# Eight column blocks in PSUM at once for the first products of a two-layer encoder, slice by slice of the depth, with no GpSimd work

## The chip, the cores and the metric

The kernel runs on one core of a Trainium2 chip. The time is the device time of one execution in microseconds (us); the time before is the median of three runs, 1584.74 us (1583.31 to 1587.51).

## The reference, cut to what matters

The model is a two-layer encoder trunk over 256 tokens of width 1024 in float32. Each layer has a feed-forward half step, a mixer of three branches and a second feed-forward half step. Each of the three is fed by a normalised and modulated input. The modulation is a product of a conditioning vector with a large weight matrix `ada_w`.

```python
cs = jax.nn.silu(c)                                   # c: (1, 1024)
mod = cs @ ada_w[l] + ada_b[l]                        # nine vectors of 1024
sh1, sc1, gt1, sh2, sc2, gt2, sh3, sc3, gt3 = jnp.split(mod, 9, axis=-1)
h = rmsnorm(x, norm_gains[l, 0]) * (1 + sc1) + sh1
gate, up = jnp.split(h @ ffn_wi[l, 0], 2, axis=-1)    # 1024 -> 2 x 2816
x = x + 0.5 * gt1 * ((jax.nn.silu(gate) * up) @ ffn_wo[l, 0])
h = rmsnorm(x, norm_gains[l, 1]) * (1 + sc2) + sh2    # the mixer's input
```

## The kernel before, in words

Everything is kept transposed: depth on the partitions, 256 tokens along the free dimension. The depth of 1024 is eight slices k of 128. The 2816 columns of `gate` and of `up` are 22 column blocks j of 128. Each product of a 128x128 weight tile with a slice of the activations is three matmuls (`mm3`, lines 396 to 398), since both factors are split into a rounded high part and the remainder, hi and lo. ScalarE rounds the weights to the high part, VectorE subtracts to get the low part.

The order of the instructions on each engine is written by a planner in the kernel itself (class `Order`). The kernel is a set of Python generators. Each says on which engine it wants to work and how long that takes by the planner's own figures (`yield on("DVE", 1.13)`), which events it waits for, and which counted buffers it takes. The thread that could start first goes first, and among equals the one with the lower priority number. What comes out is a fixed order per engine; on the chip each engine runs its list in order and waits by semaphores. The load queue (SP) is such a list too, planned at 1.45 us a load, landing 2 us after.

The first products, lines 682 to 783, are h @ ffn_wi for the first `NJ0` = 6 column blocks of layer 0, which run while the modulation of this very input is still being computed. For slice k, `ada_w` blocks k (shift) and 8+k (scale) of 128x1024 are needed, 512 KB each, multiplied with the replicated conditioning vector `csb` and summed along the row. VectorE does this for the scales and for shift 7 (line 460, one fused instruction with a reading of its accumulator). For the other seven shifts GpSimd multiplies (line 700) and ScalarE sums (line 702). The list `FIRST` gives the order of the loads: a single number k is the pair of modulation blocks of a slice (shift first, scale second, except for slice 7), a pair (j, q) is half q of the depth, four slices, of column block j with its gate and up columns, 512 KB. So a column block is usable for slices 0 to 3 when its first half has come, and for 4 to 7 when its second has. `first_put` (line 736) multiplies x with the row norm (line 740), applies scale and shift on ScalarE (line 744), and rounds and subtracts in `ha.put` (lines 419, 421). Each pair (slice, block) is multiplied, six triplets a slice for gate and six for up, as soon as both its inputs are planned to be there. The six blocks take six of the eight PSUM banks.

After the first products `ffn` goes on with the other column blocks through the stream `wraw`, `whi`, `wlo` (lines 337, 352, 361), into the PSUM tiles `pmain`. At the end of the first products it also starts the `ada` thread: 24 further modulation blocks, layer 0's vectors 2, 4 and 3, at 12, 17, 22 ... us of planner time after that moment (`FSTART`, `FPACE`). Vector 3 comes last. It is the shift of the mixer's input: `Stats.scale` waits for all of it (line 521), writes it into two extra columns of the early activations (lines 525, 526), and only then sets `e_x`, for which every early product of the mixer waits (`Stats.early`, line 536; the products into `pearly`).

Of the kernel before, what the change touches and what calls it, by code (L numbers as in the profile page):

```python
# [9 lines left out]
F32R = mybir.dt.float32r  # L10
I32 = mybir.dt.int32
U8 = mybir.dt.uint8
AF = mybir.ActivationFunctionType
OP = mybir.AluOpType

L, D, S, H, HD, W = 2, 1024, 256, 8, 64, 512
KT = D // 128
# [8 lines left out]
NRAW, NSPL, NADA, NPM = 3, 4, 2, 3  # L26
ORDER = "cabAgB"
NCK, NLR = 2, 2
WARM = 0
NJ0, SHV = 6, (7,)  # L30
FIRST = ((0,), (0, 0), (1, 0), (2, 0), (3, 0), (4, 0), (1,), (5, 0), (2,), (0, 1), (1, 1), (3,), (2, 1), (3, 1), (4,), (4, 1), (5,), (5, 1), (6,), (7,))
NXF, NXM = 4, 8
PACE, START = 7, 110
FPACE, FSTART = 5, 12
# [1 line left out]
LAT, MM = {"PE": 0.2, "ACT": 0.15, "DVE": 0.13, "SP": 0.0}, 0.329  # L36
# [122 lines left out]
def on(eng, dur, lat=None, tab=None):  # L159
    return ("on", eng, dur, LAT[eng if isinstance(eng, str) else eng[0]] if lat is None else lat, tab)  # L160


def wait(ev):
    return ("wait", ev, 0, 0)
# [6 lines left out]
def take(sem, n=1):  # L171
    return ("take", sem, n, 0)
# [15 lines left out]
def trunk(ctx, tc, A, out):  # L188
    nc = tc.nc
    V, S_, P = nc.vector, nc.scalar, nc.tensor  # L190
# [7 lines left out]
    od = Order()  # L198
    s_raw, s_spl, s_ada = Sem(NRAW), Sem(NSPL), Sem(NADA)
    s_pm, s_px, s_big = Sem(NPM), Sem(8 - NPM), Sem(NBIG)  # L200
# [6 lines left out]
    def paux(name, shape=(128, 512)):  # L207
        return ps.tile(list(shape), F32, name=name, tag="bank", bufs=8)

    def big(name, shape=(128, 4, S), dt=F32):  # L210
        return act.tile(list(shape), dt, name=name, tag="b4", bufs=NBIG)
# [7 lines left out]
    def free_big(n=1):  # L219
        od.release(s_big, n)  # L220


    def cload(key, shape, dt=F32, eng=nc.scalar):
        t = const.tile(list(shape), dt, name="c_" + key)
        eng.dma_start(t, A[key])
        return t

    xT = act.tile([128, KT, S], F32, name="xT")
    csb = const.tile([128, D], F32, name="csb")
# [5 lines left out]
    ada_b = cload("ada_b", [128, L, 72])  # L235
# [11 lines left out]
    for q in range(2):  # L247
        p = paux("pc")
# [58 lines left out]
    for l in range(L):  # L307
# [6 lines left out]
        for q in ORDER:  # L314
            t, b0, b1 = parts[q]
# [79 lines left out]
    def mm3(o, w, xh, xl, first, last):  # L395
        P.matmul(o, w[0], xh, start=first, stop=False)  # L396
        P.matmul(o, w[0], xl, start=False, stop=False)  # L397
        P.matmul(o, w[1], xh, start=False, stop=last)  # L398
# [52 lines left out]
    modT = [const.tile([128, 72], F32, name=f"modT{l}") for l in range(L)]  # L451
# [3 lines left out]
    have1 = [Event() for _ in range(16)]  # L455

    def ada_block(l, blk, raw, got, paced):
        yield wait(got)
        yield on("DVE", 1.14)
        V.tensor_tensor_reduce(out=raw, in0=raw, in1=csb, scale=0.5, scalar=0.0, op0=OP.mult, op1=OP.add,  # L460
                               accum_out=modT[l][:, blk:blk + 1])
        free_big()
        if paced:
            od.release(s_ada)
        v = blk // 8
        if l == 0 and v < 2:
            yield on("DVE", 0.07)
            m, b = modT[0][:, blk:blk + 1], ada_b[:, 0, blk:blk + 1]
            if v == 0:
                V.tensor_add(m, m, b)  # L470
            else:
                V.scalar_tensor_tensor(m, m, b, gains[:, 0, blk - 8:blk - 7], op0=OP.add, op1=OP.mult)
            od.set(have1[blk])
            return
        left[l, v] -= 1
        if left[l, v] == 0:
            yield on("DVE", 0.08)
            V.tensor_add(mod(l, v), mod(l, v), ada_b[:, l, v * 8:v * 8 + 8])
            od.set(have[l, v])

    def ada_load(l, blk, prio, paced=True):
        if paced:
            yield take(s_ada)
        yield take(s_big)
        raw = big("araw", (128, D))
        yield on("SP", 1.45, 0.0)
        nc.sync.dma_start(raw, A["ada_w"][l, blk])
        got = Event()
        od.set(got, 2.0)
        od.spawn(ada_block(l, blk, raw, got, paced), prio)  # L490
# [152 lines left out]
    def ffn_evac(j, p, za, sem=s_pm):  # L643
        yield take(s_z)
        z = small("ffz")
        yield on("ACT", 0.264, tab="exp")
        S_.activation(z, p[:, 0], AF.Tanh, scale=0.5)
        yield on("DVE", 0.34)
        V.scalar_tensor_tensor(z, z, 1.0, p[:, 0], op0=OP.add, op1=OP.mult)
        yield on("DVE", 0.34)  # L650
        V.tensor_mul(z, z, p[:, 1])  # L651
        od.release(sem)
        yield from za.put(j, z)
        od.release(s_z)
# [24 lines left out]
        yield from za.put(j, z)  # L679
        od.release(s_z, 3)  # L680

    w0 = {(j, q): Event() for j in range(NJ0) for q in range(2)}
    raws0 = {q: Event() for q in w0}

    def first_weights(j, q, raw):
        yield take(s_big, 2)
        hi, lo = (big("w0" + n, (128, 2, 512), F32R) for n in "hl")
        yield wait(raws0[j, q])
        yield on("ACT", 0.94)
        S_.copy(hi, raw)  # L690
        yield on("DVE", 1.13)
        V.tensor_tensor(lo, raw, hi, op=OP.subtract)
        free_big()
        w0[j, q].w = hi, lo
        od.set(w0[j, q])

    def first_shift(k, raw, got):
        yield wait(got)
        yield on("POOL", 2.3, 0.2)
        nc.gpsimd.tensor_tensor(out=raw, in0=raw, in1=csb, op=OP.mult)  # L700
        yield on("ACT", 1.05)
        S_.activation(raw, raw, AF.Copy, scale=0.5, accum_out=modT[0][:, k:k + 1])
        free_big()
        yield on("DVE", 0.07)
        V.tensor_add(modT[0][:, k:k + 1], modT[0][:, k:k + 1], ada_b[:, 0, k:k + 1])
        od.set(have1[k])

    def first_mod(k):
        if k in SHV:
            yield from ada_load(0, k, 1, False)  # L710
            yield from ada_load(0, 8 + k, 1, False)
            return
        yield take(s_big)
        raw, got = big("raw0", (128, D)), Event()
        yield on("SP", 1.45, 0.0)
        nc.sync.dma_start(raw, A["ada_w"][0, k])
        od.set(got, 2.0)
        od.spawn(first_shift(k, raw, got), 1)
        yield from ada_load(0, 8 + k, 1, False)

    def first_loads():

        for x in FIRST:
            if len(x) == 1:
                yield from first_mod(x[0])
                continue
            j, q = x
            yield take(s_big)
            raw = big("w0raw", (128, 2, 512))
            yield on("SP", 1.45, 0.0)  # L730
            nc.sync.dma_start(raw, A["ffn_wi"][0, 0, j].rearrange("p (s q c) -> p s q c", s=2, q=2)[:, :, q])
            od.set(raws0[j, q], 2.0)
            od.spawn(first_weights(j, q, raw), 2)
        od.set(e_w)

    def first_put(k, ha):
        yield take(s_z)
        t = small("ht")
        yield on("DVE", 0.34)
        V.tensor_mul(t, xT[:, k], first.r)  # L740
        yield wait(have1[8 + k])
        yield wait(have1[k])
        yield on("ACT", 0.4)
        S_.activation(t, t, AF.Identity, scale=modT[0][:, 8 + k:9 + k], bias=modT[0][:, k:k + 1])
        yield from ha.put(k, t)
        od.release(s_z)

    def first_modulated(ha):
        yield on("DVE", 0.07)
# [4 lines left out]
        first.used()  # L754

    def first_products(ha):

        sems = [s_px] * min(NJ0, 4) + [s_pm] * (NJ0 - 4)
        for q in sems:
            yield take(q)  # L760
        ps0, za = [paux("pfirst", (128, 2, 256)) for _ in range(NJ0)], None
        at_ = {tuple(x): i for i, x in enumerate(FIRST)}
        jobs = sorted((max(at_[k,], at_[j, k // 4]), k, j) for k in range(KT) for j in range(NJ0))
        n, left0 = [0] * NJ0, [4 * NJ0] * 2
        for _, k, j in jobs:
            n[j] += 1
            if k == KT - 1 and za is None:
                yield take(s_big, 12)
                za = Act("z", NJ)
            yield wait(w0[j, k // 4])  # L770
            hi, lo = w0[j, k // 4].w
            for s in range(2):
                c = slice(k % 4 * 128, k % 4 * 128 + 128)
                if ha.ev[k].t is None or ha.ev[k].t > od.cur.t:
                    yield wait(ha.ev[k])
                yield on("PE", MM, 0.0)
                mm3(ps0[j][:, s], (hi[:, s, c], lo[:, s, c]), ha.hi(k), ha.lo(k), n[j] == 1 and s == 0, n[j] == KT and s == 1)
            if n[j] == KT:
                od.spawn(ffn_evac(j, ps0[j], za, sems[j]), 1)
            left0[k // 4] -= 1  # L780
            if left0[k // 4] == 0:
                free_big(2 * NJ0)
        return za

    def ffn(l, f, n, st, lvs, nxt):
# [973 lines left out]
    first = Stats((0, 0))  # L1759
# [148 lines left out]
```

## Time and profile before

| what | us |
|---|---|
| median of three runs | 1584.74 |
| the profiled execution's own time | 1586.35 |
| its span, first to last instruction | 1584.6 |
| TensorE busy in the span | 1533.1 (97%) |
| VectorE busy | 1311.7 (83%) |
| ScalarE busy | 897.0 (57%) |
| GpSimd busy | 21.3 (1%) |

The times in all views are us from the start of the span. A view of windows gives for each engine the busy time in a stretch (x is the number of instructions), then the TensorE clock granted by the throttle as a share of 2.4 GHz, then the load of the DMA engines and what they moved. PE is TensorE, DVE is VectorE, ACT is ScalarE, POOL is GpSimd, SPq the load queue. A duration of an instruction includes its fill; instructions overlap, so the step from one start to the next is what an instruction costs in a row of them.

### The profile page before, as it was taken

How to read it: one execution, taken by the hardware profiler on the slowest of the kernel's cores; microseconds unless marked ns; L12 is line 12 of the kernel's file. 1: busy time of each engine (PE TensorE's matmuls, PEld its weight loads, DVE VectorE, ACT ScalarE, POOL GpSimd, SP SyncE). 2: the span in 40 equal slices, each digit the busy share in tenths (PEclk: the TensorE clock that was granted, in tenths of full speed). 3: DMA queues.
4: the chain of work that ended last, by engine and by line, in shares of the span. 5: the costliest groups of instructions: out<-in, count | busy, mean ns of one | idle time of the engine just before them, and what ended most of it. 6: DMA issues, size and time to landing. Idle time of an engine off the chain costs nothing.

```text
span 1584.6 us, 36797 instructions
## 1 busy us (share of the span) xinstructions
PE 1533.1 (97%) x14518; PEld 1450.6 (92%) x14518; DVE 1311.7 (83%) x2938; ACT 897.0 (57%) x1854; POOL 21.3 (1%) x29
## 2 busy tenths in 40 slices
PE   3999999999999989999999999999999999999998
PEld 3999999988888889999999999998888987999997
DVE  7878889989888869997779877898888896888664
ACT  4655567576554447554565545676655445565554
POOL 3100000000000000000000000000000000000000
PEclk7999999999999989999999999999999999899999
DMA  8588864545464225888657876544446422467553
GB/s 310 188 293 272 284 230 163 180 130 198 140 230 140 74 80 174 277 287 273 226 200 272 285 266 203 185 159 155 160 159 232 168 102 68 136 202 274 184 184 127
DMA packets 91621, 311.61 MB, mean 197 GB/s; under 512 B 11444, under 2 KB 14772, under 8 KB 91448
## 3 DMA queue, kind: packets, MB, share of 16 engines
q1 hardware_dynamic: 91160, 309.15, 57.8%
q8 instruction: 114, 1.87, 0.5%
q14 instruction: 59, 0.48, 0.1%
q10 hardware_dynamic: 288, 0.10, 0.0%
HBM read 308.17 MB, written 1.05 MB: 195 GB/s over the span
## 4 chain that ended last, share of the span: by engine, by line
PE 88%; DMA 5%; DVE 4%; issue 1%; ACT 1%; SPq 0%; DVEq 0%; ACTq 0%
PE pmain L396 21%; PE pmain L397 20%; PE pmain L398 20%; DMA araw<-in_ada_w_dram 5%; PE pearly L396 2%; PE pearly L398 2%; PE pearly L397 2%; PE pX L1175 2%; PE pT L1186 2%; PE pG L1158 1%; PE pS L1488 1%; PE po L1528 1%; DVE wlo L361 1%; PE pmain L1645 1%; PE pmain L1647 1%
## 5 line engine op out<-in xcount | busy, mean ns | idle before, releaser
L352 ACT CAST whi<-wraw 128x512 fp32r<-128x512 f32 x836 | 511.9, 619 | 427.3 <-PE pmain L397 256.0
L361 DVE TENSOR_TENSOR wlo<-wraw,whi 128x512 fp32r<-128x512 f32 x836 | 571.7, 688 | 118.7 <-ACT whi L352 109.2
L396 PE MATMUL pmain<-h,whi 128*128 128x256 f32 x1872 | 539.2, 288 | 0.0
L398 PE MATMUL pmain<-h,wlo 128*128 128x256 f32 x1872 | 525.2, 281 | 1.1 <-DVE wlo L361 1.1
L397 PE MATMUL pmain<-h,whi 128*128 128x256 f32 x1872 | 525.2, 281 | 0.0
L396 PEld LDWEIGHTS pmain<-h,whi 128*128 128x128 f32 x1872 | 351.7, 188 | 13.3 <-issue 4.6
L398 PEld LDWEIGHTS pmain<-h,wlo 128*128 128x128 f32 x1872 | 352.2, 188 | 1.6 <-DVE wlo L361 1.6
L397 PEld LDWEIGHTS pmain<-h,whi 128*128 128x128 f32 x1872 | 352.3, 188 | 0.4
L460 DVE CUSTOM_DVE_ANT_0 araw<-araw,csb 128x1024 f32<-128x1024 f32 x137 | 169.0, 1235 | 47.6 <-DMA araw<-in_ada_w_dram 47.2
L398 PE MATMUL pmain<-z,wlo 128*128 128x256 f32 x704 | 198.2, 282 | 3.4 <-DVE wlo L361 3.3
L397 PE MATMUL pmain<-z,whi 128*128 128x256 f32 x704 | 197.9, 281 | 0.0
L396 PE MATMUL pmain<-z,whi 128*128 128x256 f32 x704 | 197.8, 281 | 0.0
L398 PEld LDWEIGHTS pmain<-z,wlo 128*128 128x128 f32 x704 | 132.6, 188 | 4.4 <-DVE wlo L361 4.2
L396 PEld LDWEIGHTS pmain<-z,whi 128*128 128x128 f32 x704 | 132.6, 188 | 0.0
L397 PEld LDWEIGHTS pmain<-z,whi 128*128 128x128 f32 x704 | 132.6, 188 | 0.0
L396 PE MATMUL pearly<-xh,whi 128*128 128x258 f32 x320 | 91.4, 286 | 0.0
L398 PE MATMUL pearly<-xh,wlo 128*128 128x258 f32 x320 | 90.4, 282 | 0.0
L397 PE MATMUL pearly<-xl,whi 128*128 128x258 f32 x320 | 90.2, 282 | 0.0
L397 PEld LDWEIGHTS pearly<-xl,whi 128*128 128x128 f32 x320 | 60.6, 189 | 0.0
L396 PEld LDWEIGHTS pearly<-xh,whi 128*128 128x128 f32 x320 | 60.4, 189 | 0.0
L398 PEld LDWEIGHTS pearly<-xh,wlo 128*128 128x128 f32 x320 | 60.3, 189 | 0.0
L419 ACT CAST z<-ffz 128x256 fp32r<-128x256 f32 x76 | 30.7, 405 | 40.3 <-DVE ffz L651 39.9
(306 smaller groups left out, 2459.2 us busy)
## 6 DMA issues: line engine op xcount, KB each, us to landing
wraw<-in_ffn_wi_dram SPq DMA_DIRECT2D x164, 512.0 KB, 4.9
araw<-in_ada_w_dram SPq DMA_DIRECT2D x137, 512.0 KB, 6.4
wraw<-in_ffn_wo_dram SPq DMA_DIRECT2D x88, 512.0 KB, 4.5
wraw<-in_w_in_dram SPq DMA_DIRECT2D x78, 512.0 KB, 3.7
wraw<-in_w_gb_dram SPq DMA_DIRECT2D x72, 512.0 KB, 4.2
wraw<-in_w_out_dram SPq DMA_DIRECT2D x16, 512.0 KB, 3.6
w0raw<-in_ffn_wi_dram SPq DMA_DIRECT2D x12, 512.0 KB, 9.8
raw<-in_ada_w_dram SPq DMA_DIRECT2D x7, 512.0 KB, 7.9
```

The source lines that it names most:

```text
L352: S_.copy(hi, part(q))
L361: V.tensor_tensor(lo, part(q), hi, op=OP.subtract)
L396: P.matmul(o, w[0], xh, start=first, stop=False)
L397: P.matmul(o, w[0], xl, start=False, stop=False)
L398: P.matmul(o, w[1], xh, start=False, stop=last)
L419: S_.copy(self.hi(k), src)
L460: V.tensor_tensor_reduce(out=raw, in0=raw, in1=csb, scale=0.5, scalar=0.0, op0=OP.mult, op1=OP.add, accum_out=modT[l][:, blk:blk + 1])
L1158: P.matmul(pp[b][:, i], BK[d][i // 2][hs, i % 2, c].rearrange("p a b -> p (a b)"), ar_view(d, i // 2)[hs, :, i % 2, cs_], start=True, stop ...
L1175: P.matmul(px[half(h), h // 2], G[half(h), h // 2, h % 2, 0:64], T[half(h), h // 2], start=True, stop=True)
L1186: P.matmul(pt[half(h), h // 2], X[half(h), h // 2], TT[half(h), h // 2], start=True, stop=True)
L1488: P.matmul(pS[e][:, t], qT[half(e), hp, t * 128:(t + 1) * 128], kT[half(e), hp], start=True, stop=True)
L1528: P.matmul(po[half(e)], vv[:, j, (2 * hp + e) * 64:(2 * hp + e + 1) * 64], pt_[:, 2 * e + j], start=j == 0, stop=j == 1)
```

## The change

The first products take eight column blocks, a PSUM bank each, and go slice by slice. The loads are one regular sequence: for each slice the scale and the shift block of `ada_w`, and at every even slice four loads of weights. Load (g, i) holds slices 2g and 2g+1 of four column blocks, of gate (i even) or up (i odd): 1 KB per partition and block, four blocks, 512 KB as before. Both modulation blocks are reduced on VectorE by line 460's instruction, at priority 0; the GpSimd and ScalarE code for the shifts is gone. `first_put` works as the other stages' code does: scale and norm in one VectorE instruction, shift and rounding in one on ScalarE, the low part in one on VectorE. All eight PSUM banks are taken as the products come to them.

```diff
-NJ0, SHV = 6, (7,)
-FIRST = ((0,), (0, 0), (1, 0), (2, 0), (3, 0), (4, 0), (1,), (5, 0), (2,), (0, 1), (1, 1), (3,), (2, 1), (3, 1), (4,), (4, 1), (5,), (5, 1), (6,), (7,))
+NJ0 = 8
...
-    def first_weights(j, q, raw):
-        yield take(s_big, 2)
-        hi, lo = (big("w0" + n, (128, 2, 512), F32R) for n in "hl")
-        yield wait(raws0[j, q])
+    def first_weights(g, i, raw):
+        hi, lo = (big("w0" + n, (128, 1024), F32R) for n in "hl")
+        yield wait(raws0[g, i])
         yield on("ACT", 0.94)
         S_.copy(hi, raw)
         yield on("DVE", 1.13)
         V.tensor_tensor(lo, raw, hi, op=OP.subtract)
...
-    def first_shift(k, raw, got):
-        yield wait(got)
-        yield on("POOL", 2.3, 0.2)
-        nc.gpsimd.tensor_tensor(out=raw, in0=raw, in1=csb, op=OP.mult)
-        yield on("ACT", 1.05)
-        S_.activation(raw, raw, AF.Copy, scale=0.5, accum_out=modT[0][:, k:k + 1])
...
     def first_loads():
...
+        for k in range(KT):
+            yield from ada_load(0, 8 + k, 0, False)
+            yield from ada_load(0, k, 0, False)
+            for i in range(0 if k % 2 else NJ0 // 2):
+                yield take(s_big, 3)
+                raw = big("w0raw", (128, 1024))
+                yield on("SP", 1.45, 0.0)
+                j0, c0 = i // 2 * 4, i % 2 * 1024 + 128 * k
+                nc.sync.dma_start(raw.rearrange("p (j c) -> p j c", j=4),
+                                  A["ffn_wi"][0, 0, j0:j0 + 4].rearrange("j p c -> p j c")[:, :, c0:c0 + 256])
+                od.set(raws0[k // 2, i], 2.0)
+                od.spawn(first_weights(k // 2, i, raw), 2)
         od.set(e_w)

     def first_put(k, ha):
+        yield wait(have1[8 + k])
         yield take(s_z)
         t = small("ht")
-        yield on("DVE", 0.34)
-        V.tensor_mul(t, xT[:, k], first.r)
-        yield wait(have1[8 + k])
+        yield on("DVE", 0.4)
+        V.scalar_tensor_tensor(t, xT[:, k], modT[0][:, 8 + k:9 + k], first.r, op0=OP.mult, op1=OP.mult)
         yield wait(have1[k])
+        sh = modT[0][:, k:k + 1]
         yield on("ACT", 0.4)
-        S_.activation(t, t, AF.Identity, scale=modT[0][:, 8 + k:9 + k], bias=modT[0][:, k:k + 1])
-        yield from ha.put(k, t)
+        S_.activation(ha.hi(k), t, AF.Identity, bias=sh)
+        yield on("DVE", 0.396)
+        V.scalar_tensor_tensor(ha.lo(k), t, sh, ha.hi(k), op0=OP.add, op1=OP.subtract)
...
     def first_products(ha):
-
-        sems = [s_px] * min(NJ0, 4) + [s_pm] * (NJ0 - 4)
-        for q in sems:
-            yield take(q)
-        ps0, za = [paux("pfirst", (128, 2, 256)) for _ in range(NJ0)], None
...
+        sems = [s_pm] * NPM + [s_px] * (NJ0 - NPM)
+        ps0, za = [], None
+        for k in range(KT):
+            if k == KT - 1:
                 yield take(s_big, 12)
                 za = Act("z", NJ)
...
+            for i in range(NJ0 // 2):
+                yield wait(w0[k // 2, i])
+                hi, lo = w0[k // 2, i].w
+                for j in range(i // 2 * 4, i // 2 * 4 + 4):
+                    if ha.ev[k].t is None or ha.ev[k].t > od.cur.t:
+                        yield wait(ha.ev[k])
+                    if k == 0 and i % 2 == 0:
+                        yield take(sems[j])
+                        ps0.append(paux("pfirst", (128, 2, 256)))
+                    yield on("PE", MM, 0.0)
+                    mm3(ps0[j][:, i % 2], (hi[:, j % 4, k % 2], lo[:, j % 4, k % 2]), ha.hi(k), ha.lo(k),
+                        k == 0 and i % 2 == 0, k == KT - 1 and i % 2 == 1)
+                    if k == KT - 1 and i % 2 == 1:
+                        od.spawn(ffn_evac(j, ps0[j], za, sems[j]), 1)
+                if k % 2 == 1:
+                    free_big(2)
         return za
```

## Rows read from the trace of the kernel before

**Rows 1.** The page, busy time of each engine over the span
```profile
PE 1533.1 (97%) x14518; PEld 1450.6 (92%) x14518; DVE 1311.7 (83%) x2938; ACT 897.0 (57%) x1854; POOL 21.3 (1%) x29
```
**Rows 2.** Windows: stretch, length, PE, PEld, DVE, ACT, POOL, clock, DMA share, GB/s
```profile
20.00:45.00 25.00, 14.79 (x87) 13.90 (x88) 24.07 (x31) 12.75 (x21) 10.69 (x5) 0.71 0.79 286
45.00:62.00 17.00, 17.00 (x143) 16.66 (x142) 16.39 (x29) 10.41 (x20) 4.17 (x2) 1.00 0.61 222
```
**Rows 3.** Waits of PE, 0 to 80 us: total, times, longest
```profile
PE pfirst L396 <- ACT h L419: 9.5, 2, 6.8
```
**Rows 4.** Timeline of ACT, 34 to 37 us: start, busy, what
```profile
35.25 0.60 ACT L744 ACTIVATE ht<-ht,modT 128x256 f32<-128x256 f32 x1 [10.11 <-DVE modT L472]
```
**Rows 5.** Timeline of DVE, 0 to 75 us
```profile
18.72 7.08 DVE L740 TENSOR_TENSOR ht<-xT,rs 128x256 f32<-128x256 f32 x8
25.72 1.21 DVE L692 TENSOR_TENSOR w0l<-w0raw,w0h 128x1024 fp32r<-128x1024 f32 x1
26.85 0.41 DVE L421 TENSOR_TENSOR h<-ht,h 128x256 fp32r<-128x256 f32 x1
...
28.32 3.41 DVE L460 CUSTOM_DVE_ANT_0 araw<-araw,csb 128x1024 f32<-128x1024 f32 x1
...
41.30 1.22 DVE L460 CUSTOM_DVE_ANT_0 araw<-araw,csb 128x1024 f32<-128x1024 f32 x1
...
42.56 0.22 DVE L472 SCALAR_TENSOR_TENSOR modT<-modT,c_ada_b,c_gains 128x1 f32<-128x1 f32 x1
42.70 0.15 DVE L705 TENSOR_TENSOR modT<-modT,c_ada_b 128x1 f32<-128x1 f32 x1
42.77 1.22 DVE L692 TENSOR_TENSOR w0l<-w0raw,w0h 128x1024 fp32r<-128x1024 f32 x1
```
**Rows 6.** Timeline of POOL, 0 to 75 us
```profile
9.00 2.38 POOL L700 TENSOR_TENSOR raw<-raw,csb 128x1024 f32<-128x1024 f32 x1 [8.57 <-DMA raw<-in_ada_w_dram]
...
27.52 3.13 POOL L700 TENSOR_TENSOR raw<-raw,csb 128x1024 f32<-128x1024 f32 x1 [2.68 <-DMA raw<-in_ada_w_dram]
```
**Rows 7.** The chain that ended last, 0 to 40 us: start, length, what
```profile
9.29 2.38 DVE sqacc L566
...
12.83 0.44 DVE sqacc L566
```
**Rows 8.** Tile pfirst: count, duration min/median/max in ns, first and last start
```profile
L398 PE MATMUL pfirst<-h,w0l x96: 275/281/420, 27.7 to 69.0; 128*128 128x256 f32 x96
```
**Rows 9.** Timeline of PE, 69 to 72.5 us (24 matmuls from one to the other)
```profile
69.12 0.28 PE L396 MATMUL pmain<-h,whi 128*128 128x256 f32 x1
...
71.94 0.28 PE L396 MATMUL pmain<-h,whi 128*128 128x256 f32 x1
```
**Rows 10.** Timeline of SP, 0 to 80 us: issues of 256 and of 128 pieces
```profile
10.18 0.55 SPq L731 DMA_DIRECT2D w0raw<-in_ffn_wi_dram  x1
11.63 0.33 SPq L716 DMA_DIRECT2D raw<-in_ada_w_dram  x1
```
**Rows 11.** Tile h, 200 to 240 us: the same low part in a later stage
```profile
L638 DVE SCALAR_TENSOR_TENSOR h<-ht,modT,h x3: 475/476/480, 233.6 to 239.9; 128x256 fp32r<-128x256 f32 x3
```
**Rows 12.** Windows of 5 us, columns as in rows 2
```profile
25.00:30.00 5.00, 2.68 (x12) 2.68 (x13) 5.00 (x7) 0.15 (x1) 2.48 (x1) 0.50 1.04 399
30.00:35.00 5.00, 2.95 (x19) 2.54 (x17) 5.00 (x5) 0.00 (x0) 2.79 (x2) 0.89 0.57 224
35.00:40.00 5.00, 3.58 (x20) 3.38 (x21) 4.58 (x9) 4.72 (x8) 0.20 (x1) 0.79 0.41 116
```
**Rows 13.** Tile pearly, 0 to 400 us: the mixer's early products
```profile
L396 PE MATMUL pearly<-xh,whi x64: 278/283/364, 224.3 to 248.2; 128*128 128x258 f32 x64
```
**Rows 14.** Tile araw, 60 to 260 us: issues of the 24 further blocks
```profile
L487 SPq DMA_DIRECT2D araw<-in_ada_w_dram x24: 377/425/1361, 82.8 to 207.8; - x24
```
**Rows 15.** Timeline of DVE, 206 to 222 us: the last of the shift columns
```profile
217.06 0.17 DVE L526 TENSOR_TENSOR xl<-modT,xh 128x8 fp32r<-128x8 f32 x1
```

More of the change, by code (lines that the diff above doesn't have):

```diff
@@ L680, in ffn_evac_early @@
         od.release(s_z, 3)
-    w0 = {(j, q): Event() for j in range(NJ0) for q in range(2)}
+    w0 = {(g, i): Event() for g in range(KT // 2) for i in range(NJ0 // 2)}
     raws0 = {q: Event() for q in w0}
-    def first_weights(j, q, raw):
-        yield take(s_big, 2)
-        hi, lo = (big("w0" + n, (128, 2, 512), F32R) for n in "hl")
-        yield wait(raws0[j, q])
+    def first_weights(g, i, raw):
+        hi, lo = (big("w0" + n, (128, 1024), F32R) for n in "hl")
+        yield wait(raws0[g, i])
         yield on("ACT", 0.94)
@@ L693, in first_weights @@
         free_big()
-        w0[j, q].w = hi, lo
-        od.set(w0[j, q])
-    def first_shift(k, raw, got):
-        yield wait(got)
-        yield on("POOL", 2.3, 0.2)
-        nc.gpsimd.tensor_tensor(out=raw, in0=raw, in1=csb, op=OP.mult)
-        yield on("ACT", 1.05)
-        S_.activation(raw, raw, AF.Copy, scale=0.5, accum_out=modT[0][:, k:k + 1])
[L703 to L719, printed above, removed]
-    def first_loads():
[L723 to L733, printed above, removed]
+        w0[g, i].w = tuple(t.rearrange("p (j k c) -> p j k c", j=4, k=2) for t in (hi, lo))
@@ new lines, in first_weights @@
+        od.set(w0[g, i])
+    def first_loads():
+        for k in range(KT):
[10 more added lines that the diff above has]
+                od.spawn(first_weights(k // 2, i, raw), 2)
@@ L745, in first_put @@
-        yield from ha.put(k, t)
+        S_.activation(ha.hi(k), t, AF.Identity, bias=sh)
+        yield on("DVE", 0.396)
+        V.scalar_tensor_tensor(ha.lo(k), t, sh, ha.hi(k), op0=OP.add, op1=OP.subtract)
         od.release(s_z)
+        od.set(ha.ev[k])
     def first_modulated(ha):
@@ L756, in first_products @@
     def first_products(ha):
-        sems = [s_px] * min(NJ0, 4) + [s_pm] * (NJ0 - 4)
-        for q in sems:
-            yield take(q)
-        ps0, za = [paux("pfirst", (128, 2, 256)) for _ in range(NJ0)], None
[L762 to L767, printed above, removed]
+        sems = [s_pm] * NPM + [s_px] * (NJ0 - NPM)
+        ps0, za = [], None
+        for k in range(KT):
+            if k == KT - 1:
                 yield take(s_big, 12)
                 za = Act("z", NJ)
[L770 to L782, printed above, removed]
+            for i in range(NJ0 // 2):
[14 more added lines that the diff above has]
+                    free_big(2)
         return za
```

## The prediction

> **What bounds the kernel now.** I read the page first: TensorE is busy 97% of the span, VectorE 83%, GpSimd 21 us [rows 1]. So what counts is when TensorE has no work or runs slowly. The windows put nearly all of that at the start: from 45 us it is full and its clock at 1.00, while from 20 to 45 us it is busy 14.8 of 25 us and starts 87 instructions; VectorE is full in both [rows 2]. The waits name the missing input: the first matmul of a slice waits for ScalarE's h [rows 3], and ScalarE itself sat idle 10.1 us for VectorE's finished modulation [rows 4]. VectorE's timeline tells why it is late. Eight products of 128x256 took 7.08 us, and one reduction 3.41 us where its fellow takes 1.22 [rows 5]. Each long one lies beside a GpSimd multiplication of 2.4 to 3.1 us [rows 6]; so does the addition of 2.38 us in the chain, where the others take 0.44 [rows 7]. VectorE, held up by GpSimd, bounds the first 41 us.
>
> The first products' 288 matmuls end at 69.1 us, the next stage following at once [rows 8, 9]. A matmul costs 2.82/24 = 0.1175 us there [rows 9]. The 96 more that the change moves into this stage are done at 69.12 + 11.28 = **80.4 us**. That is the mark: the same 384 matmuls, before and after.
>
> **The change, part by part.**
>
> *Removed from GpSimd and ScalarE, added to VectorE.* Seven shift reductions move to VectorE, at 1.26 us each up to the dependent step (41.30 to 42.56), and its own steps after a reduction are 0.14 (scale) and 0.07 (shift) [rows 5]. That is 8.8 us more VectorE work. In return its two-input operations run undisturbed: the third addition gives back 2.38 - 0.44 = 1.9 us, so the six end at 12.83 + 0.44 - 1.9 = 11.3 us [rows 7]. ScalarE loses seven sums and eight casts; nothing waits for what replaces them.
>
> *Modulation.* Scale and norm in one VectorE step, low part in another. The later stage's low part lasts 0.476 us, 0.06 more than the present one [rows 5, 11], which steps in about 0.34, so 0.40 each. The ScalarE step between I take at today's 0.60 [rows 4].
>
> *Weights.* Sixteen low parts of 1.13 us instead of twelve (25.72 to 26.85) [rows 5]; the four more replace eight of the ordinary stream.
>
> *VectorE's list.* The planner's figures give only the order. With the rows' durations, for the first slice: additions to 11.3, two reductions 13.8, small steps 14.2, about 0.4 for ScalarE's first rounding, two low weight parts 16.8, slice 0's scaling 17.2, a third weight part, then slice 0's low part, at **18.8 us**; fourth weight part 19.9. Slice 1: two reductions, a small step, one of slice 2's reductions, scaling, two small steps, slice 2's other reduction, low part: 26.1. From then on two slices cost VectorE 4 x 1.26 + 0.42 + 4 x 1.13 + 4 x 0.40 = 11.6 us, so slice 3 is ready at 37.7, slice 5 at 49.3, and slice 7, with no successors' work before it, at 58.8.
>
> *TensorE.* Two slices are 96 matmuls, 11.3 us. It starts in earnest at 18.8. Today it starts so at 27.3, at 0.50 of its clock (1.2 GHz), 12 matmuls in 2.68 us; the clock of 0.89 over the next window leaves about 1.1 us of it at that level [rows 12]. Some 17 matmuls, about 0.1 us dearer each: 1.8 us. Slice 0 is done at 18.8 + 5.6 + 1.8 = 26.2, slice 1 at 31.9, slice 2 at 37.5; slice 3 starts at 37.7, slice 5 at 49.3, and slice 7 ends at **66.2 us**, 1.8 us of slack on its input. Gain at the mark: 80.4 - 66.2 = **14.2 us**.
>
> *Loads.* Blocks of load 0 and load 14 are awaited by GpSimd at 9.00 and 27.52 [rows 6], so a load takes 18.52/14 = 1.323 us; eight of those fourteen were weights in 2 KB pieces. The 32 loads end at 9.0 + 31 x 1.323 = 50.0 us; slice 7's last block is needed by 57.7 if TensorE is not to wait, 7.7 us later. Issuing 256 pieces takes 0.55 us and 128 take 0.33 [rows 10]; 512 would take 0.99 (an estimate from these), hidden under 1.32. The trace has no load in 1 KB pieces: between unchanged and growing as the issue does, threefold, I take unchanged, since the issue's extra 0.22 us did not show in the pace. Buffers free in VectorE's order well ahead of the loads that take them.
>
> *PSUM.* All eight banks are taken. The first four blocks are complete eight triplets, 2.8 us, before the stage ends, so a bank comes free in time; I cost it at nothing. Without that cover the next stage would wait for one evacuation, a ScalarE and two VectorE steps of 0.4 to 0.6 us [rows 4, 5], some 1.5 us.
>
> *What is late next.* The 24 further modulation blocks are planned from the end of this stage, the last issued 207.8 - 69.1 = 138.7 us after it, its shift columns written at 217.2, 148.1 us after [rows 14, 15]. The mixer's early products, which wait for them, start 224.3 - 69.1 = 155.2 us after, 7.1 us later than that [rows 13]. With two column blocks fewer behind the mark they would start at 155.2 - 11.3 = 143.9 us: **4.2 us before the columns are there**. The planner's due times do not move, so a new wait appears. Bounds 0 and 4.2; I take 4.0, as load and reduction stay tied to the same distance. A pause in TensorE's work also costs clock: in the window with its second stop for h, 9.5 - 6.8 = 2.7 us long, the mean is 0.79, so 2.1 us at half clock, 1.05 us lost there [rows 3, 12]. Between 0 and 1.8 I take 1.0.
>
> *Elsewhere* every planned instant moves, and threads can change places in the mixers. No row shows the price; between -4 and +4 us I take 0.
>
> **The sum.** 14.2 - 4.0 - 1.0 = 9.2 us. The span goes from 1584.6 to 1575.4; with the 1.75 us around it the execution goes from 1586.35 to 1577.15. The median lies 1.6 us below that execution: **1575.5 us**.
>
> **Rivals.**
>
> B, *no new wait in the mixer*: the last blocks come earlier, for instance because their DMA queue is emptier then. For it: VectorE sat 7 us ahead of need before. Against it: the due times are counted from the end of the stage. All 14.2 us stay: 1570.5.
>
> C, *VectorE becomes the bound*. Its 11.6 us for two slices already exceed TensorE's 11.3. If each of some 20 instructions waits 0.1 us for its semaphore, two slices take 13.6; slice 1 is ready at 27.5, slice 7 at 65.8, the end is 71.4, and the sum loses 5.2: 1580.7. Against it: in the undisturbed stretch VectorE's instructions follow one another without gaps [rows 5].
>
> D, *the loads in 1 KB pieces, each 8 KB from the next, come slowly*, and the change loses. With more than 7.7/16 = 0.5 us extra a load they set the end of the stage, and from (7.7 + 9.2)/16 = 1.06 us extra, 2.4 us a load, it is slower than before. Priced at 3.0 us, between today's and threefold: 16 x 1.68 - 7.7 - 9.2 = +10 us, 1594.7. Against it: the eight loads in 2 KB pieces kept the pace. [...]
>
> **Chances.** Forecast 0.57, B 0.21, C 0.13, D 0.09. A measurement of this kernel tells some 0.3%, 4.75 us, from no change. Forecast and B are faster by more, C lies within, D is slower: faster 0.78, same 0.13, slower 0.09. The forecast's own range is 1571 to 1580; with B less 4 us and C plus 3 the whole is 1567 to 1584, which leaves out D and little else.
>
> **What would show it.** Right: no POOL work after the memsets; no VectorE operation of 128x1024 over 1.3 us; first products from about 18 us to 65 to 68 us with the clock full after about 23; a wait of PE of 3 to 4 us at the first `pearly` matmul, its releaser the reduction or the columns. Wrong: load spacing far above 1.32 us; waits between slices over 1 us; no wait at `pearly`; more idle time in the mixers.

## The result, and the profile after

The changed kernel took 1626.03 us (median of four runs, 1623.78 to 1627.65) against 1584.93 us (1583.31 to 1587.51) for the kernel before: ratio 1.0256, 95% interval 1.024 to 1.0272. It is **slower by 41 us**, where 9 us faster was forecast. The lines of the code have moved: the triplet is now L395 to L397, the reduction L459, the low part of the first weights L692.

The page of the kernel after, busy time and two of its 40-slice lines (a slice is 40.55 us):

```profile
PE 1552.5 (96%) x14518; PEld 1465.7 (90%) x14518; DVE 1314.6 (81%) x2954; ACT 884.8 (55%) x1820; POOL 2.3 (0%) x22
...
PE   6999999999868998999999999999999999899997
...
PEclk8999999999887998999999999999999999899999
```

Compare [rows 1]. The matmuls are the same 14518, GpSimd's multiplications are gone (2.3 us of clearing memory stay), and yet TensorE is busy 19 us longer: part of its work now runs at a lower clock. The place is plain in both 40-slice lines, in slices 11 to 13 and 16, about 405 to 530 and 610 to 650 us, far behind the code that was changed.

**The first stage did what was forecast.** Windows of the kernel after, columns as in [rows 2], then the tile `pfirst` and the next stage's first matmul:

```profile
20.00:45.00 25.00, 25.00 (x195) 25.00 (x196) 24.93 (x46) 9.73 (x12) 0.00 (x0) 0.91 1.06 374
45.00:62.00 17.00, 17.00 (x145) 17.00 (x145) 14.09 (x27) 8.77 (x12) 0.00 (x0) 1.00 0.79 279
```
```profile
L397 PE MATMUL pfirst<-h,w0l x128: 276/280/415, 20.2 to 67.3; 128*128 128x256 f32 x128
```
```profile
67.40 0.28 PE L395 MATMUL pmain<-h,whi 128*128 128x256 f32 x1
```

TensorE is full from 20 us, where it stood idle 10 of 25 us before [rows 2]. The next stage's first matmul starts at 67.40 us; before, the same 384 matmuls were done at 80.4 (the mark). VectorE's timeline after gives the reason:

```profile
18.16 1.22 DVE L692 TENSOR_TENSOR w0l<-w0raw,w0h 128x1024 fp32r<-128x1024 f32 x1
19.30 0.48 DVE L724 SCALAR_TENSOR_TENSOR h<-ht,modT,h 128x256 fp32r<-128x256 f32 x1
19.69 1.22 DVE L459 CUSTOM_DVE_ANT_0 araw<-araw,csb 128x1024 f32<-128x1024 f32 x1
...
25.00 0.48 DVE L724 SCALAR_TENSOR_TENSOR h<-ht,modT,h 128x256 fp32r<-128x256 f32 x1
...
36.11 0.48 DVE L724 SCALAR_TENSOR_TENSOR h<-ht,modT,h 128x256 fp32r<-128x256 f32 x1
```

These are the low parts of slices 0, 1 and 3. With no GpSimd work beside it the reduction takes 1.22 us, not the 3.41 of [rows 5].

**The new wait is there too.** VectorE, then TensorE, then windows, all of the kernel after, at the step into the mixer:

```profile
210.81 1.23 DVE L459 CUSTOM_DVE_ANT_0 araw<-araw,csb 128x1024 f32<-128x1024 f32 x1 [1.18 <-DMA araw<-in_ada_w_dram]
...
212.57 0.48 DVE L586 SCALAR_TENSOR_TENSOR xT<-pmain,g,xT 128x256 f32<-128x256 f32 x1
```
```profile
213.95 0.38 PE L600 MATMUL pss<-ones,sq 128*128 128x1 f32 x2 [2.64 <-ACT sq L556]
...
214.64 0.36 PE L395 MATMUL pearly<-xh,whi 128*128 128x258 f32 x1
```
```profile
210.00:215.00 5.00, 2.36 (x22) 2.27 (x21) 3.80 (x11) 1.93 (x5) 0.00 (x0) 1.00 0.62 192
215.00:220.00 5.00, 5.00 (x32) 5.00 (x31) 3.04 (x12) 2.42 (x7) 0.00 (x0) 0.66 0.27 97
220.00:225.00 5.00, 5.00 (x44) 5.00 (x44) 4.52 (x10) 3.59 (x8) 0.00 (x0) 1.00 0.54 168
```

VectorE waits 1.18 us for the last modulation block. Behind that block in its list stands the last residual update (L586), which the norm's sums on TensorE need, and the early products are queued behind those sums. TensorE stands 2.64 us and then gets a clock of 0.66 in a window with 32 matmuls where the next holds 44.

**The loss comes after that.** The tile `pearly` occurs at the head of each stage that makes early products; a gap is the time from the first early product of one stage to that of the next, and the mixer's gap is called its length. Kernel after, its first two groups; then the second group of the kernel before (its first is [rows 13]):

```profile
L395 PE MATMUL pearly<-xh,whi x64: 279/283/419, 214.6 to 239.2; 128*128 128x258 f32 x64
...
L395 PE MATMUL pearly<-xh,whi x64: 279/283/367, 654.2 to 678.1; 128*128 128x258 f32 x64
```
```profile
L396 PE MATMUL pearly<-xh,whi x64: 278/283/364, 614.9 to 638.7; 128*128 128x258 f32 x64
```

The mixer of layer 0 begins 9.7 us earlier than before and ends 39.3 us later: 439.6 us from group to group, where it was 390.6. The three gaps that follow are the same within 2.5 us (190.2, 189.2, 390.5 after; 189.5, 191.7, 390.5 before). So **one mixer of two takes 49 us more**, though none of its code was touched. Windows within it, the kernel after and the kernel before:

```profile
360.00:400.00 40.00, 40.00 (x440) 38.04 (x440) 25.42 (x59) 18.23 (x37) 0.00 (x0) 1.00 0.40 124
400.00:460.00 60.00, 53.02 (x477) 44.70 (x475) 47.67 (x119) 29.22 (x74) 0.00 (x0) 0.91 0.44 149
460.00:520.00 60.00, 38.31 (x502) 30.23 (x497) 49.93 (x139) 15.98 (x38) 0.00 (x0) 0.80 0.51 165
520.00:600.00 80.00, 79.89 (x1146) 70.39 (x1145) 55.61 (x163) 33.51 (x75) 0.00 (x0) 0.92 0.20 68
600.00:620.00 20.00, 12.93 (x166) 10.94 (x163) 6.26 (x17) 5.35 (x12) 0.00 (x0) 0.62 0.08 27
```
```profile
360.00:400.00 40.00, 39.04 (x336) 34.35 (x336) 35.49 (x87) 24.02 (x55) 0.00 (x0) 1.00 0.57 195
400.00:460.00 60.00, 58.26 (x660) 49.84 (x657) 50.43 (x129) 33.31 (x86) 0.00 (x0) 1.00 0.52 176
460.00:520.00 60.00, 60.00 (x909) 53.31 (x909) 54.16 (x161) 27.82 (x61) 0.00 (x0) 1.00 0.48 165
...
370.00:410.00 40.00, 39.51 (x415) 35.49 (x416) 34.77 (x90) 22.05 (x54) 0.00 (x0) 1.00 0.48 156
```

From 360 to 400 us TensorE runs 440 matmuls where it ran 336, and VectorE only 59 instructions where it ran 87. (At the same distance from the mixer's head, the last line, the kernel before ran 415 and 90.) The large products run ahead, while VectorE's chains (attention, scan) stand still. From 400 to 520 us those chains run with little beside them; TensorE waits between their steps, and its granted clock falls to 0.91 and then 0.80 on the mean, where it was 1.00. The three longest waits of TensorE, 240 to 620 us, after, and what the same places waited before:

```profile
PE p L1198 <- DVE m L1193: 10.4, 3, 6.3
PE pX L1151 <- DVE txw L1214: 7.5, 8, 2.5
PE pPT L1495 <- DVE w L1204: 5.2, 1, 5.2
```
```profile
PE p L1222 <- DVE m L1217: 1.9, 2, 0.9
...
PE pX L1175 <- DVE txw L1238: 0.8, 1, 0.8
```

What stood still shows in the loads of `bt`, the attention bias of one of the branches. After, then before:

```profile
L1455 SPq DMA_DIRECT2D bt<-in_bt_dram x8: 327/428/1177, 401.5 to 464.5; - x8
```
```profile
L1479 SPq DMA_DIRECT2D bt<-in_bt_dram x8: 328/426/1461, 364.2 to 426.2; - x8
```

The first comes 186.9 us after the first early product, where it came 139.9 us after: 47 us late, nearly the whole loss. A `bt` load is issued when its thread has a *big* buffer for it. There are 32 (`NBIG`), counted, shared by all threads.

**Theory (hold-up).** The planner keeps the account of these buffers. The trace has no such count; the following is the planner's own account, worked out from the code of the kernels, in us of planner time. The bias branch of `attend` takes two buffers for its probabilities, then a third for each bias. In the kernel before, buffers that come free from 328 us on reach the scan's threads first, then the thread of the large products and an attention thread, which gets all three; these finish and give theirs back, and the second attention thread follows. In the kernel after, two buffers are free at 326 us, and the thread of the large products takes both at once (for its merged result). The next ones leave both attention threads with two each and waiting for a third, while the last step of the scan's preparation (`finish`) has none. From 330.4 to 372.3 us nobody returns any, until the products' thread gives two back; in no other kernel of this study does such a stretch that begins between 295 and 470 us last over 18.5 us.

In the plan, what tips the order is when the modulation blocks that are loaded during the mixer come. They are planned from the moment at which the stage before has no more work for TensorE (`START` us after it, then every `PACE` us). That moment is 4.8 us earlier in the plan after, but the mixer's threads are only 2.5 us earlier: the new wait stands in the plan too and parts the two by 2.3 us.

**Rivals:** the mixer is dearer on the chip because of the new wait and the half clock at its head; or an engine or the load queue is late in it; or such edits to the mixer help either kernel.

### The profile page after: what moved, and what is told of

Same layout as the page of the kernel before. It is cut to its first block, busy times and chain, and to the rows that moved or that the text cites. A ratio compares the mean times of both kernels' runs of the same rounds, so it can differ in the third digit from the quotient of the medians.

```text
span 1622.0 us, 36786 instructions
## 1 busy us (share of the span) xinstructions
PE 1552.5 (96%) x14518; PEld 1465.7 (90%) x14518; DVE 1314.6 (81%) x2954; ACT 884.8 (55%) x1820; POOL 2.3 (0%) x22
## 4 chain that ended last, share of the span: by engine, by line
PE 88%; DVE 5%; DMA 4%; issue 1%; ACT 1%; SPq 0%; DVEq 0%; ACTq 0%
PE pmain L395 21%; PE pmain L396 20%; PE pmain L397 20%; PE pearly L395 2%; PE pearly L396 2%; PE pearly L397 2%; DMA araw<-in_ada_w_dram 2%; PE pX L1151 2%; PE pT L1162 2%; DVE araw L459 1%; PE pG L1134 1%; PE po L1504 1%; PE pfirst L396 1%; PE pS L1464 1%; PE pfirst L397 1%
## 5 line engine op out<-in xcount | busy, mean ns | idle before, releaser
L395 PE MATMUL pmain<-h,whi 128*128 128x256 f32 x1840 | 532.3, 289 | 0.0
L396 PE MATMUL pmain<-h,whi 128*128 128x256 f32 x1840 | 520.5, 283 | 0.0
L397 PE MATMUL pmain<-h,wlo 128*128 128x256 f32 x1840 | 518.4, 282 | 0.1
L395 PEld LDWEIGHTS pmain<-h,whi 128*128 128x128 f32 x1840 | 348.4, 189 | 13.9 <-issue 5.4
L396 PEld LDWEIGHTS pmain<-h,whi 128*128 128x128 f32 x1840 | 348.6, 189 | 0.4
L397 PEld LDWEIGHTS pmain<-h,wlo 128*128 128x128 f32 x1840 | 348.4, 189 | 0.4 <-DVE wlo L360 0.3
L459 DVE CUSTOM_DVE_ANT_0 araw<-araw,csb 128x1024 f32<-128x1024 f32 x144 | 175.0, 1219 | 39.4 <-DMA araw<-in_ada_w_dram 39.4
L397 PE MATMUL pmain<-z,wlo 128*128 128x256 f32 x704 | 197.8, 281 | 1.1 <-DVE wlo L360 1.1
L395 PE MATMUL pmain<-z,whi 128*128 128x256 f32 x704 | 197.5, 281 | 0.0
L397 PEld LDWEIGHTS pmain<-z,wlo 128*128 128x128 f32 x704 | 132.6, 188 | 1.8 <-DVE wlo L360 1.8
L395 PEld LDWEIGHTS pmain<-z,whi 128*128 128x128 f32 x704 | 132.5, 188 | 0.0
L395 PE MATMUL pearly<-xh,whi 128*128 128x258 f32 x320 | 92.2, 288 | 0.0
L397 PE MATMUL pearly<-xh,wlo 128*128 128x258 f32 x320 | 91.1, 285 | 0.0
L396 PEld LDWEIGHTS pearly<-xl,whi 128*128 128x128 f32 x320 | 61.4, 192 | 0.0
L395 PEld LDWEIGHTS pearly<-xh,whi 128*128 128x128 f32 x320 | 61.2, 191 | 0.0
L397 PEld LDWEIGHTS pearly<-xh,wlo 128*128 128x128 f32 x320 | 61.2, 191 | 0.0
```

## The experiments

The kernel before ran beside each batch on the same chip: 1581.9, 1583.1, 1583.3 and 1583.7 us. Ratios are to it.

**1. After, with the three buffers claimed in one step (`e1_claim`).**

```diff
-            yield take(s_big, 2)
+            yield take(s_big, 2 + br)
...
-                    yield take(s_big)
+                    if hp != hps[0]:
+                        yield take(s_big)
```

> The changed kernel; only the attention of branch B now claims its three buffers at once (two for probabilities, one for the bias), where it took two and then waited for the third while holding them. First stage and load times untouched. Theory (the 47 us are lost because two attention threads hold two buffers each and wait for a third in the order written by the planner): layer 0's mixer is as short as before, the first bias load comes about 140 us after the first early product again (187 in the changed kernel), the wait at the early products stays (2 to 4 us), total 1575 us (1570 to 1582). Rival 1 (the new first stage slows the mixer on the chip itself: clock, loads, VectorE): 1615 to 1630. Rival 2 (the new wait of TensorE at the early products sets the mixer back): the wait is still there, so 1615 to 1630.

Measured 1589.03 us, ratio 1.0027 (1.0007 to 1.0047). Its `pearly`, first and second group:

```profile
L395 PE MATMUL pearly<-xh,whi x64: 279/283/419, 214.7 to 239.3; 128*128 128x258 f32 x64
...
L395 PE MATMUL pearly<-xh,whi x64: 277/282/367, 616.7 to 640.3; 128*128 128x258 f32 x64
```

The head of the mixer is the same as in the kernel after, the wait and the slow clock included, yet the mixer takes 402.0 us instead of 439.6. So 38 of 49 us hung on how these buffers are claimed; 11 remained, though the mixer was expected to be as short as before. The ten executions lie in two groups, four from 1580.8 to 1583.6 us and six from 1588.7 to 1591.8, and the trace is of the upper one; how much of the 11 belongs to that isn't shown.

**2. After, with the ordinary modulation blocks of every feed-forward half step paced 4.9 (`e2_fpace`);** the 24 ahead of the mixer of layer 0 are those that count here.

```diff
-FPACE, FSTART = 5, 12
+FPACE, FSTART = 4.9, 12
```

> The changed kernel; only the 24 modulation blocks after the first products are due every 4.9 instead of every 5 us, so the last is planned 2.3 us earlier. Theory: the wait at the early products goes (2.3 us and the half clock after it, some 4 us in all), and with the mixer's start moved the buffers are claimed in another order, without two holders waiting for each other: 1570 us (1564 to 1577). Rival 1: the mixer stays slow, 1612 to 1628. Rival 2: as the theory here, about 1570.

Measured 1571.72 us, ratio 0.9931 (0.9911 to 0.9952), the fastest kernel of this study and faster than both. TensorE's one wait at the mixer's head (205 to 225 us), then the first two groups of `pearly`:

```profile
PE pearly L395 <- DVE xh L524: 0.8, 1, 0.8
```
```profile
L395 PE MATMUL pearly<-xh,whi x64: 277/284/366, 213.1 to 237.3; 128*128 128x258 f32 x64
...
L395 PE MATMUL pearly<-xh,whi x64: 276/283/365, 602.9 to 626.8; 128*128 128x258 f32 x64
```

The wait is down from 2.64 to 0.8 us, and the mixer is back at 389.8 us. But two things moved at once: the wait, and with it the distance from the loads beside the mixer to the mixer's threads, which in this plan is that of the kernel before again (all of it 4.8 us earlier). This run can't tell whether the wait counts on the chip or through the plan; experiments 5 and 12 can, where the wait stays.

**3. Before, with the loads of the mixer two units later (`e3_before_start112`).**

```diff
-PACE, START = 7, 110
+PACE, START = 7, 112
```

> The kernel before, first stage and all; only the modulation blocks that are loaded during the mixer are due from 112 instead of 110 us after its start. Theory: the first 240 us are the same to a few tenths; the claims on the buffers of layer 0's mixer fall in another order with a holder that waits, and that mixer becomes 25 to 45 us longer: 1605 to 1632. Rivals 1 and 2: nothing of the first stage or of the early products is changed, so 1583 to 1588.

Measured 1611.79 us, ratio 1.018 (1.0153 to 1.0208). The mixers take 407.8 and 401.8 us instead of 390.6 and 390.5; so the total came out as expected, but not by one mixer 25 to 45 us longer. The first `bt` load is issued in its usual place, and the plan has no stretch like that of the kernel after; what is late in these two mixers is not shown. The kernel before has no change of its first stage and no new wait, and loses some 28 us to a due time moved by two. The price of a moved instant, which the prediction set within 4 us, is of that size.

**4. Before, with all shifts reduced on VectorE (`e4_before_nopool`): the GpSimd part of the change alone, with the ScalarE sums that belong to it.**

```diff
-NJ0, SHV = 6, (7,)
+NJ0, SHV = 6, (0, 1, 2, 3, 4, 5, 6, 7)
```

> The kernel before with one part of the change: all eight shift reductions go to VectorE, none to GpSimd; six column blocks and the order of the loads stay. If taking GpSimd away is what speeds the first stage: VectorE gains about 13 us of blocked time and takes 8.8 us of reductions, first products end at 64 to 67 us (69.1 before), total 1578 to 1583. If the order slice by slice and the eight blocks do it: no VectorE instruction is stretched any more, but the first products still end at 68 to 72 us, total 1584 to 1588.

Measured 1575.35 us, ratio 0.9953 (0.9939 to 0.9967). Its `pfirst`:

```profile
L398 PE MATMUL pfirst<-h,w0l x96: 276/282/582, 20.4 to 61.4; 128*128 128x256 f32 x96
```

The 288 matmuls end at 61.4 us instead of 69.0 [rows 8]. Brought to the mark of 384 that is 61.5 + 11.3 = 72.8 us: 7.6 of the 13.0 us at the mark are GpSimd's going, more than was expected. The other 5.4 are left for the eight blocks, the regular order and the shorter `first_put`, which no run separates. The mixers keep their 390.5 and 390.4 us.

**5 and 6. Both kernels with START 125 (`e5_after_start125`, `e6_before_start125`).** The same line as in experiment 3, with 125.

> The kernel after, with the modulation loads that run beside a mixer set 15 us later (START 125 for 110). Nothing before the mixer is touched, so first products (18.8 to 67.3) and the first early product (214.6, with its wait of 2 to 4 us) stay. Hold-up theory (at START 110 the loads free a big buffer just in time for the wrong thread, and both attention threads then sit on two buffers each): layer 0's mixer, 439.6 us from one early product to the next, comes back to 386 to 396, first bias load about 140 us after the first early product; total 1571 to 1580. Rival (the change itself makes the mixer dearer, by the wait at the early products and the half clock behind it, whatever the order): the mixer stays above 425 us, total over 1610.

> The kernel before with the same later modulation loads (START 125): the partner of the run above, so that the change can be judged with both kernels at a setting that neither was fitted to. First products 23 to 69, first early product 224. Hold-up theory: no thread is caught here, mixer of layer 0 390 to 396 us, total 1583 to 1594; the change is then worth about its first stage, 8 to 14 us, between the two runs. Rival (the loss of the change is a property of its own work): the pair differs by 35 to 45 us the other way.

Measured 1578.37 us, ratio 0.9968 (0.9956 to 0.998), and 1585.39 us, ratio 1.0016 (1.0004 to 1.0027). The kernel after with START 125, its first two groups of `pearly` and its `bt`:

```profile
L395 PE MATMUL pearly<-xh,whi x64: 279/283/366, 214.9 to 237.9; 128*128 128x258 f32 x64
...
L395 PE MATMUL pearly<-xh,whi x64: 277/282/368, 604.1 to 627.7; 128*128 128x258 f32 x64
```
```profile
L1455 SPq DMA_DIRECT2D bt<-in_bt_dram x8: 422/424/606, 351.2 to 415.0; - x8
```

The edit touches nothing ahead of the mixer: it begins at 214.9 us, still after a wait (1.8 us). The mixer takes 389.2 us and `bt` comes 136.3 us after its head. So neither the first stage nor a wait of this length makes the mixer long on the chip. With the setting changed in both kernels, the change is 0.48% faster, 7.6 us, just under the 8 to 14 that were expected.

**7 and 9. Both kernels with 34 big buffers (`e7_after_nbig34`, `e9_before_nbig34`).**

```diff
-NBIG, NZ, NZ2 = 32, 10, 2
+NBIG, NZ, NZ2 = 34, 10, 2
```

> The kernel after with 34 big buffers in place of 32, all else alike. Hold-up theory (a shortage of exactly these buffers: two attention threads hold two each and each wants a third): two more buffers end it, the mixer of layer 0 falls from 439.6 to 390 to 405 us, total 1573 to 1590. Rival (the time is lost on an engine or a DMA queue that is late, not on buffers): within 5 us of the kernel after, 1626.

> The kernel before with 34 big buffers: the partner of the kernel after with 34, which took 1582.7. Hold-up theory: with 32 no thread of the kernel before is caught, so two more buffers give it little: layer 0's mixer 384 to 395 us, total 1572 to 1586. Against the partner the first stage still ends earlier in the kernel after, but either kernel's mixers may fall out by several us either way. Rival (buffers are short in both kernels alike, and the kernel after only shows it more): this kernel gains 20 us or more, under 1563.

Measured 1582.7 us, ratio 0.9996 (0.9983 to 1.0009), and 1584.79 us, ratio 1.0007 (0.9996 to 1.0017). The second group of `pearly` in the kernel after with 34:

```profile
L395 PE MATMUL pearly<-xh,whi x64: 277/283/366, 611.4 to 635.2; 128*128 128x258 f32 x64
```

From 213.9 that is 397.5 us. Two buffers more take 42 of the 49 us back where the order had run short; the kernel before gains next to nothing by them (388.7 us, the total the same). That an engine or the queue is late in itself falls with this.

**8. Before, with the claim in one step (`e8_before_claim`).** The edit of experiment 1.

> The kernel before with the attention threads of branch B claiming their three buffers in one step, the edit of the first run. Hold-up theory: nobody is caught in the kernel before, so the edit has nothing to give: layer 0's mixer 388 to 397 us, total 1581 to 1590. Rival (the edit is a plain improvement of the mixer, and what the first run got back had nothing to do with the change): faster than before by 10 us or more, under 1572.

Measured 1590.8 us, ratio 1.0048 (1.0031 to 1.0065), the mixer 394.4 us. The edit is no improvement in itself: it costs the kernel before 4 us in this mixer. So 4 of the 11 us that remained in experiment 1 may be its own price and 1.4 the slow clock at the head; the rest isn't explained.

**10. Before, with pace 4.9 (`e10_before_fpace`).** The edit of experiment 2.

> The kernel before with the 24 ordinary modulation blocks paced 4.9 instead of 5 (the edit of the second run of the first batch): its partner, 1571.7. It has 7 us of slack on the last of those blocks, so there is no wait to take away: first early product 222 to 226, layer 0's mixer 388 to 397, total 1579 to 1592; the change is then worth 8 to 18 us between the pair, more than with START 125, since here its new wait is gone too. Rival (the pace itself is what helps): this kernel drops to about 1575 as well.

Measured 1582.13 us, ratio 1.0001 (0.999 to 1.0011): the pace gives the kernel before nothing, and the pair with experiment 2 differs by 0.70%, 11.1 us.

**11. After, pace 4.9, one claim, START 107 (`e11_after_fpace_claim`): a try for a faster version.** The diffs of experiments 1 and 2, and START 107.

> The kernel after with three edits together: pace 4.9, the attention threads' three buffers claimed in one step, START 107. A try for a version faster than pace 4.9 alone (1571.7). If the single claim costs by itself what it cost the kernel before (about 6 us), the total is 1572 to 1579; if that was only the order it happened to give, 1566 to 1572. Layer 0's mixer 385 to 395 us, first early product 213 to 214.

Measured 1576.42 us, ratio 0.9953 (0.9935 to 0.9971), the mixer 394.2 us. Slower than pace 4.9 alone, by about what one claim cost in experiment 8.

**12. After, with START 112 (`e12_after_start112`),** partner of experiment 3.

> The kernel after with START 112: the partner of the kernel before with START 112, which lost 27 us in its two mixers without any change of the first stage. Theory (the mixers' length is a draw of the planned order, which the change and any due time deal anew; it does not belong to the change): layer 0's mixer comes back from 439.6 to under 400 us with two units of START, the first stage and the first early product stay at 67 and 214.6; layer 1's mixer may be long instead, as in the partner; total 1575 to 1612, at or under the partner's 1611.8. Rival (the change itself pushes the mixer over an edge, whatever the draw): layer 0's mixer stays above 425 us and the total above 1615.

Measured 1589.88 us, ratio 1.0038 (1.0024 to 1.0051). Its second group of `pearly`:

```profile
L395 PE MATMUL pearly<-xh,whi x64: 278/284/367, 603.9 to 627.8; 128*128 128x258 f32 x64
```

From 212.5 that is 391.4 us: two units of START, which bring the loads back to within 0.4 us of their old distance from the mixer's threads in the plan, and the 49 us are gone. The stop at the mixer's head (2.37 us) and the slow clock behind it are still there:

```profile
215.00:220.00 5.00, 5.00 (x36) 5.00 (x36) 3.51 (x8) 3.32 (x7) 0.00 (x0) 0.79 0.07 25
```

So the first rival falls. Layer 1's mixer has grown to 407.1 us instead, for a reason that was not traced. Either kernel can draw a good or a bad order for either mixer.

All pairs, each kernel with the same setting (difference in per cent of the kernel before, and in us):

| setting of both | before | after | change is worth |
|---|---|---|---|
| as given | 1 | 1.0256 | +2.56%, +41 |
| START 112 | 1.0180 | 1.0038 | -1.42%, -22 |
| START 125 | 1.0016 | 0.9968 | -0.48%, -7.6 |
| 34 buffers | 1.0007 | 0.9996 | -0.11%, -1.7 |
| pace 4.9 | 1.0001 | 0.9931 | -0.70%, -11.1 |
| one claim | 1.0048 | 1.0027 | -0.21%, -3.3 |

The intervals of the two kernels overlap for 34 buffers and for one claim, so these two differences are not clear of the noise. In each pair the mixer's head comes 9 to 12 us earlier after the change. What the mixers make of it goes either way.

## Why the prediction was wrong

- **First slice and end of the stage: right.** Forecast 18.8 us and 66.2, measured 18.8 (first matmul) and 67.4; the gain at the mark 13.0 us, forecast 14.2. Between 20 and 45 us TensorE did 195 matmuls where 25/0.1175 = 213 would fit: 18 lost to the slow clock, forecast 17.
- **VectorE's list: right.** Low parts of slices 1 and 3 start at 25.00 and 36.11, forecast done 26.1 and 37.7. Rival C fell: TensorE does not wait between slices.
- **Loads: a little off, no effect.** Eight loads took 23.88 - 12.69 = 11.19 us, 1.40 us each against 1.323. SP's timeline after:

```profile
12.69 7.48 SPq L707 DMA_DIRECT2D w0raw<-in_ffn_wi_dram  x4
20.22 3.57 SPq L486 DMA_DIRECT2D araw<-in_ada_w_dram  x4
23.88 7.45 SPq L707 DMA_DIRECT2D w0raw<-in_ffn_wi_dram  x4
```

  The issue of a weight load, estimated at 0.99 us, took 0.41 in the median (3.14 at most). Four of them are stretched to some 7.5 us, but the blocks came in time. Rival D fell: 374 GB/s were moved between 20 and 45 us.
- **The new wait: right in kind and nearly in size.** From the mark to the early products 214.64 - 67.40 = 147.2 us against 143.9 without it: 3.3 us, forecast 4.0. Its path was another: the block held up VectorE's list, in which the residual update stood behind it, and the last of the columns was written at the same moment (214.52 us). The slow clock cost 12 matmuls, 12 x 0.1175 = 1.4 us, forecast 1.0. What the forecast did not see is that this wait also moves the mixer's threads against the loads planned beside them.
- **The step that failed: "Elsewhere every planned instant moves, and threads can change places in the mixers. No row shows the price; between -4 and +4 us I take 0."** The terms above leave 13.0 - 3.3 - 1.4 = 8.3 us of gain, forecast 9.2. The span of the profiled executions grew by 1622.0 - 1584.6 = 37.4 us, so "elsewhere" is +45.7 us. By the gaps: 49.0 - 1.4 = 47.6 in layer 0's mixer, -1.9 in all the rest. The bound of 4 us rested on no row, and the range and the chances stood on it.
- What the runs showed in its place: the instant at which the mixer's side loads are planned decides who gets a big buffer when they are short, and the wrong turn cost the kernel after 49 us in one mixer. (START 112 made three other mixers 11 to 17 us longer; that the buffers are the cause there too is not shown.) That these buffers are the cause in the kernel after is shown twice, by the number (34) and by the way of claiming (one step), with the control that neither helps the kernel before. That the planned instant brings it about is shown by START 112 and 125, with the wait still there; that it was the new wait which had moved it is read from the plan, and pace 4.9 agrees. Which threads held which buffers is worked out from the planner's code, not seen on the chip. What makes up the last 7 us of the mixer with 34 buffers is open.
- The prediction's own sign for being wrong, more idle time in the mixers, came up; no rival had it as its mechanism.

## What to carry to other kernels

Where an order is planned from due times and counted buffers, a local gain is worth what the planner makes of it: before judging an edit, measure both kernels at several settings of the due times, since the one kernel may be at a setting fitted to it. Read the planner's own end first: it is 1460 us for the kernel before and 1522 for the kernel after, 1505 and 1495 for the two with START 112, and 1449 to 1468 for the ten others here. So a loss of this size stood in the plan before anything ran, where the forecast took 0 for want of a row. (The 402 us of experiment 1 do not show in it.) A thread that takes two buffers and asks for a third later can stop everybody, and the place where that shows is far from the edit: compare the gaps between like stages before reading instructions. A bound in a sum needs a row behind it, or it must be as wide as the stage it speaks of.

## What was not expected of the hardware

- A stop of TensorE of 2.6 to 3.0 us at the mixer's head, with only the norm's sums over single columns between it and the first early product, was followed by a clock of 0.66 or 0.67 in the next 5 us window (the kernel after, one claim, 34 buffers). With START 112 the stop was 2.37 us and the clock 0.87 in the window that holds it and 0.79 in the next. In the kernel after with START 125 the stop was 1.8 us, and the clock stayed at 1.00:

```profile
215.00:220.00 5.00, 5.00 (x43) 5.00 (x44) 4.27 (x15) 3.48 (x8) 0.00 (x0) 1.00 0.31 104
```

  Between a stop of 2.64 and one of 1.8 us that window differs by 11 matmuls, 1.3 us.
- Eight loads of 512 KB, four of them weights in pieces of 1 KB with four blocks 1 MB apart, went at 1.40 us each; with weights in 2 KB pieces, eight of fourteen, a load took 1.32 us, six per cent less. The two stretches differ in more than the pieces.
